# The compression operand laid out position by position and written by engines, and attention's order drawn from new seeds

## The chip, the cores and the metric

One core of a Trainium2 chip runs the whole program: two layers of a decoder trunk on 256 tokens of width 1024. The metric is the device time of one execution in microseconds (us), as the median of several runs. The engines are TensorE (PE in the profile, PEld for its weight loads), VectorE (DVE), ScalarE (ACT), GpSimd (POOL) and SyncE (SP), which in this kernel only issues DMAs. Each engine works through its own queue of instructions in the order in which the program emitted them, and waits by semaphores for the others.

## The reference, cut to what matters

Layer 0 is a recurrent mixer and an MLP, layer 1 is sparse attention and an MLP, and a norm follows. The change lies in layer 1's attention, in the compression of keys and values:

```python
def _compress(z, pe, w1, w2):                 # z: 256 tokens, 4 groups, 64 wide
    chunks = z.reshape(B, n_chunk, CMP_STRIDE, G, DH)                  # 16 chunks of 16 tokens
    blocks = jnp.concatenate([chunks[:, r:r + nc] for r in range(CMP_RATIO)], axis=2)   # 15 blocks of 32
    blocks = blocks + pe[None, None, :, None, :]
    flat = jnp.transpose(blocks, (0, 1, 3, 2, 4)).reshape(B, nc, G, CMP_LEN * DH)
    return jax.nn.gelu(flat @ w1, approximate=True) @ w2
...
    k_c = _compress(kv[:, :, 0], pe_k, w1_k, w2_k)
    v_c = _compress(kv[:, :, 1], pe_v, w1_v, w2_v)
...
        s_c = jnp.einsum('qghd,ngd->ghqn', qf, kc) - slopes * d_c.astype(jnp.float32)
        p_c = _masked_softmax(s_c, d_c >= 0)
        o_c = jnp.einsum('ghqn,ngd->qghd', p_c, vc)
...
        o = g[..., 0:1] * o_c + g[..., 1:2] * o_s + g[..., 2:3] * o_w
```

## The kernel before

The activations stay on chip, transposed: `xt` holds 8 chunks of 128 features by 256 tokens. Almost every product is taken as three passes over operands split into a high and a low part (`mm3`, L328 to L330), with a weight of 128 rows and 256 moving columns. Weights stream from memory in pieces of 128x1024 fp32: SP loads a piece into one of 5 raw buffers (L274), ACT or DVE casts the high part (L288, L336), DVE subtracts to get the low part (L297, L333). Seven split pieces are held in `whl`. Eight pieces of attention go another way, through POOL's queue: a DMA into the high part (L388), a negation (L390) and an accumulating DMA (L392).

The attention stage is a section of its own. `Section.add` records each operation with its engine (or a choice of two), an assumed duration, the keys that it reads and writes and a due time `t`. `Plan.emit` then sets the order: `priorities` adds random amounts to the due times, drawn from a list of seeds, a list schedule and six rounds of pushing work backwards and forwards follow, and the operations are emitted by the start times that come out. `HI` is such a choice: a copy or cast that ACT (0.31) or DVE (0.21) may do. So the seeds decide the order on all five queues, and which of ACT and DVE does a copy. The recurrent layer has seeds of its own; the MLPs are written in a fixed order.

The attention section projects, in this order, `ks0 kw0 q0 q1 ck0 ck1 cv0 cv1` (the early ones), then `q2`, the values `v` in 5 pieces (L1019 to L1021, which also give the branch gates `gts`), `q3 ks1 kw1 q4 q5 q6 q7`, and the output projection `o0`, `o1`. Between these stand the scores of 16 heads (L1149 and L1150 on PE, L1156 on DVE, the exponentials L1159 on ACT), the rescaling by the gates (L1178), transposes of the probabilities (L1189, with L1192 on ACT and L1193 on DVE), and their products with the values (L1214 to L1228). The chunks `q3` to `q7`, `ks1` and `kw1` are cast into one of two buffers `th`, and SP moves the halves to their partitions by DMA (L364); `tl` is the same for the low parts.

Compression: `cproj` projects `ck` and `cv` (two chunks of two groups each), multiplies by the norm's factor into `tt` (L943 on DVE), and lays the result out in `zf`, the moving operand of the first layer. `zf` has 122 columns, namely 2 (keys, values) times 60 blocks and one column with the position embedding, for each of 16 positions `l`; its upper 64 partitions hold the positions 16 to 31 of the block. In memory it is `(z l)`: a column's 16 positions lie side by side. One block of 64x240 is contiguous, and one DMA moves it: 16 in all, issued by SP (`sec.move`, L364, `zwoh<-tt` in the trace, since `zf` lies in the buffer `zwoh`). Two small DMAs bring the embeddings (L931). `hidden` then runs 16 fp32 products of 128x122, one per position, added up in one bank (L957), each reading `zf[:, :, l]`; ACT and DVE finish the gelu into `hid` (L963 to L971). `kc_out` (L978) and `vc_out` (L997) are the second layer, `compressed` the branch's scores, softmax and transposes (L1086 to L1130).

Of the kernel before, what the change touches and what calls it, by code (L numbers as in the profile page):

```python
# [28 lines left out]
NB = 15  # L29
# [4 lines left out]
LATE = "q2 v q3 ks1 kw1 q4 q5 q6 q7".split()  # L34
TE = 2.73
W1T, T1, TH, TC, T2, T3, THS, THD, THT, NEARLY = -3.89, 3.12, 0.0, 4.6, 4.94, 3.03, 13.46, 6.73, 5.46, 8
SEEDS, ROUNDS, SHIFT, MOVES, SPREAD = ((3,), (144, 22097, 77409, 21939, 78114, 80006, 60630, 7069, 62773, 82469, 25830, 79801, 92020, 84794, 19920, 86923, 46302, 34626)), 6, 1.5, 12, 3.0
HPEN, LPEN, APEN, LEAD = 0.56, 1.0, 0.0, 9.0
RPEN = 0.51
WARM = 16  # L40
# [47 lines left out]
class Plan:  # L88
# [8 lines left out]
    def add(self, eng, dur, fn=None, r=(), w=(), t=0.0, lag=None):  # L97

        if fn is None:
            eng, fn = eng, dur  # L100
        if isinstance(eng, str):
            eng = [(eng, dur, 0.0)]
        i, deps = len(self.tasks), set()
        for k in r:
            if k in self.writer:
                deps.add(self.writer[k])
            self.readers.setdefault(k, []).append(i)
        for k in w:
            deps.update(self.readers.pop(k, ()))
            if k in self.writer:  # L110
                deps.add(self.writer[k])
            self.writer[k] = i
        deps.discard(i)
        self.tasks.append((eng, fn, sorted(deps), t, lag))
# [124 lines left out]
def trunk_kernel(ctx: ExitStack, tc: tile.TileContext, x_in, vec_in, const_in, w2_in, wts, out):  # L239
    nc = tc.nc  # L240
    ctx.enter_context(tc.manual_schedule())
    pe, dve, act, pool = nc.tensor, nc.vector, nc.scalar, nc.gpsimd
# [92 lines left out]
    def copy(o, a):  # L335
        return lambda e: (e.copy if e is act else e.tensor_copy)(o, a)  # L336

    zcols = lambda x: x[:, :S]
    HI = [("act", 0.31, 0.0), ("dve", 0.21, APEN)]
# [139 lines left out]
    vec = consts.tile([P, V_N], F32, name="vec")  # L479
# [55 lines left out]
    with ExitStack() as ph:  # L535
        rg = ph.enter_context(tc.tile_pool(name="rg", bufs=1))
        sec = Section()
        add, table = sec.add, sec.table
# [18 lines left out]
        for x in FIRST.split():  # L557
            n = 1 + x.endswith("+")
# [18 lines left out]
        for k in range(KC):  # L577
            g = vec[:, V_GM + k:V_GM + k + 1]
            t = 0.6 * k - 3
            add("act", 0.4, lambda e, k=k, g=g: e.activation(hh[:, k], xt[:, k], AF.Identity, scale=g),  # L580
                r=[("xt", k), "vec0"], w=[("hh", k)], t=t)
            add("dve", 0.4, lambda e, k=k, g=g: e.scalar_tensor_tensor(
                hl[:, k], xt[:, k], g, hh[:, k].bitcast(F32), op0=OP.mult, op1=OP.subtract), r=[("xt", k), "vec0"],
                w=[("hh", k)], t=t)
# [3 lines left out]
        for q in range(4):  # L588
            for i in range(NFINE):
                w = slice(256 * q, 256 * q + 256)  # L590
                hi, lo, rw = hi_t[i][:, w], lo_t[i][:, w], raw_t[i][:, w]
                rk = [("raw0", i, q), ("raw", i)]
                t = 1.2 * q + 0.3 * i - 2.9
                add([("dve", 0.2, 0.0), ("act", 0.31, 0.5)], copy(hi, rw), r=rk, w=[("hi0", i, q)], t=t)
                add("dve", 0.34, diff(lo, rw, hi), r=rk + [("hi0", i, q)], w=[("lo0", i, q)],
                    t=t + 0.1)
        for a, b, n in ((0, 2, 2), (0, 1, 1), (4, 6, 2), (4, 5, 1), (0, 4, 1)):
            add("dve", 0.07 + 0.267 * n, lambda e, a=a, b=b, n=n: e.tensor_tensor(
                x2[:, a:a + n], x2[:, a:a + n], x2[:, b:b + n], op=OP.add), r=[("x2", b + i) for i in range(n)],
                w=[("x2", a + i) for i in range(n)], t=4 + a / 4)  # L600
# [6 lines left out]
        sp, nsp, e8, s8, s2, ac = many([P, 8], F32, "sp", 6)  # L607
# [146 lines left out]
        for m in range(8):  # L754
            wh, wl, wk = sec.weight("out", m, to + 2.65 * m)
            b = nextbank()
            z = sec.bank(("out", m), b, zcols)
# [6 lines left out]
            t = to + 2.65 * (m + 1)  # L764
# [55 lines left out]
    with ExitStack() as ph:  # L820
        at = ph.enter_context(tc.tile_pool(name="at", bufs=1))
        sec = Section()
        add, weight, proj_t, zview, table = sec.add, sec.weight, sec.proj, sec.bank, sec.table
        own_ = lambda hf: slice(hf * 64, hf * 64 + 64)
# [20 lines left out]
        zw = [at.tile([P, 8 * S], F32, name="zw" + n, tag=n) for n in ("oh", "ol")]  # L845
# [71 lines left out]

        pre = ph.enter_context(tc.tile_pool(name="ct", bufs=1))
        ZW = 61
        zf = zw[0][:, :2 * ZW * 16].rearrange("p (z l) -> p z l", l=16)  # L920
        w1 = zw[1].rearrange("p (l c) -> p l c", l=16)
        zok, wok = [("oh", j) for j in range(8)], [("ol", j) for j in range(8)]
        cb = pre.tile([P, 1], F32, name="cb")
# [4 lines left out]
        bd = osumt.rearrange("p a (j e) -> p a j e", j=4)  # L928
        for i in range(2):
            pecol = (V_PEK, V_PEV)[i]  # L930
            add("sp", 0.5, lambda e, i=i, c=pecol: e.dma_start(zf[:, ZW * i + 60], vec_in[:, c:c + 16]), r=zok,  # L931
                w=[("z", i, "p")], t=W1T, lag=2.0)
            o, ws = offs[-1] + 4 * P * 1024, slice(8 * i, 8 * i + 8)
            add("sp", 1.5, lambda e, o=o, ws=ws: e.dma_start(w1[:, ws], wts[o:o + P * 2048].rearrange(
                "(p l c) -> p l c", p=P, l=16)[:, ws]), w=wok[4 * i:4 * i + 4] + ["loads"], t=W1T, lag=2.0)
        add("pool", 0.15, lambda e: e.memset(hid, 0.0), w=["hid"], t=-5)

        def cproj(i, gp, b, t, step):
            z, zk = proj_t(("ck", "cv")[i], gp, b, t, step)
            t += 4 * step  # L940
            n = ti["n"] = ti["n"] + 1
            x, xk = tt[n % 3], ("tt", n % 3)
            add("dve", 0.34, lambda e: e.tensor_tensor(x, z(), rs, op=OP.mult), r=[zk, "rs"], w=[xk], t=t)  # L943
            for hf in range(2):
                g = gp * 2 + hf
                for j in range(2):
                    dst = zf[own_(j), ZW * i + g * NB:ZW * i + (g + 1) * NB].rearrange("p n l -> p (n l)")
                    sec.move(dst, x[own_(hf), j * 16:j * 16 + 240], [xk] + zok, [("z", i, g, j)], t + 0.5, "sp")

        def hidden(b, t):  # L950
            hp = zview("hp", b, lambda x: x[:, :2 * ZW])
# [282 lines left out]
        def out_t(half, m, b, t, step):  # L1234
            wh, wl, wk = weight("o%d" % half, m // 2, t)
            z = zview(("out", half, m), b, zcols)
            for ks in ((0, 1), (2, 3)) if half == 0 else ((0, 1), (2,), (3,)):
                def run(e, ks=ks):
                    for kk in ks:
                        o = (m % 2) * 512 + kk * P  # L1240
                        k = half * 4 + kk
                        mm3(z(), wh[:, o:o + P], wl[:, o:o + P], oh(k), ol(k), kk == 0, kk == 3)
                add("pe", 0.33 * len(ks), run, r=wk + [(n, half * 4 + kk) for n in ("oh", "ol") for kk in ks],
                    w=[("ps", b)], t=t)
                t += step * len(ks) / 2
            add("dve", 0.34, lambda e: residual(z(), m), r=[("ps", b)], w=[("xt", m)], t=t)
            return t
# [10 lines left out]
        for i, x in enumerate(EARLY):  # L1258
            te[x] = TE * i
            if x[0] == "c":  # L1260
                cproj("kv".index(x[1]), int(x[2]), i % 2, te[x], TE / 4)
            elif x[0] == "k":
                kchunk(int(x[2]), "sw".index(x[1]), i % 2, te[x], TE / 4)
            else:
                qchunk(int(x[1]), i % 2, te[x], TE / 4)
# [40 lines left out]
        for m in range(8):  # L1306
            t = out_t(1, m, (2, 3, 4, 0, 1)[m % 5], te - 2 + 1.4 * m, PJ)
# [133 lines left out]
```

## Time and profile before

| what | us |
|---|---|
| median of 3 runs | 585.29 (584.83 to 585.83) |
| the profiled execution | 585.05 |
| span of its trace | 583.3 |
| attention stage in it, from the norm's factor to the last product with the values | 269.9 to 390.3 |

The span is the stretch of the trace with work; 1.75 us of the profiled execution lie around it. Busy time of PE counts overlapping matmuls once, so a busy PE can still be slower than it could be; the distance between starts shows the pace. In the profile an fp32 product counts as two records, so the 16 products of `hidden` are 32 records on L957.

### The profile page before, as it was taken

The page shows a single profiled execution, that of the slowest core. Times are in us where ns is not written, and L with a number is a line of the kernel's source. Part 1 is how long each engine was busy: PE and PEld are TensorE (multiplying, and loading weights), DVE is VectorE, ACT ScalarE, POOL GpSimd, SP SyncE. Part 2 cuts the span into 40 slices and gives each one's busy share as a digit, 9 for nine tenths or more (in the row PEclk, how much of TensorE's full clock was granted, in tenths as well). Part 3 has the DMA queues.
Part 4 walks back from the last instruction along what each step waited for, and adds up shares of the span by engine and source line. Part 5 has one row for each costly group of instructions (what it writes and reads, how often), then busy time and mean ns, then how long its engine had stood idle before and what let it go on. Part 6 is the DMA issues. An engine that isn't in the chain of part 4 may idle for free.

```text
span 583.3 us, 12179 instructions
## 1 busy us (share of the span) xinstructions
PE 569.1 (98%) x4756; PEld 558.6 (96%) x4756; DVE 418.3 (72%) x862; ACT 354.6 (61%) x712; POOL 56.3 (10%) x69
## 2 busy tenths in 40 slices
PE   8999999999999999999999989999999999999994
PEld 7999999999999999999999988989999999999994
DVE  6999998767665645647749989999866766464432
ACT  7699674856654433437628999986865664343410
POOL 1200000000000112211011100000000000132320
PEclk8999999999999999999999999999999999999998
DMA  8943575656556565566496776433666767467402
GB/s 286 389 127 136 182 229 197 222 188 199 195 186 213 184 217 177 189 222 217 107 332 173 157 185 172 140 70 109 227 212 183 199 198 241 156 185 219 139 2 72
DMA packets 34617, 108.39 MB, mean 186 GB/s; under 512 B 4576, under 2 KB 8304, under 8 KB 34560
## 3 DMA queue, kind: packets, MB, share of 16 engines
q1 hardware_dynamic: 31632, 98.61, 51.6%
q0 software_dynamic: 2352, 8.49, 6.5%
q8 instruction: 37, 0.61, 0.4%
q10 hardware_dynamic: 576, 0.53, 0.3%
q14 instruction: 20, 0.16, 0.1%
HBM read 103.48 MB, written 1.05 MB: 179 GB/s over the span
## 4 chain that ended last, share of the span: by engine, by line
PE 88%; ACT 5%; DVE 4%; DMA 1%; issue 0%; SPq 0%; DVEq 0%; ACTq 0%
PE bank L328 27%; PE bank L329 26%; PE bank L330 26%; PE bank L690 2%; ACT pt L1159 2%; PE bank L957 1%; ACT pt L1178 1%; DMA raw<-in_dram 1%; PE bank L1189 1%; DVE ptl L1193 1%; PE bank L1019 1%; ACT pth L1192 1%; PE bank L1021 1%; PE bank L1020 1%; DVE pt L1156 1%
## 5 line engine op out<-in xcount | busy, mean ns | idle before, releaser
L328 PE MATMUL bank<-hhl,whl 128*128 128x256 f32 x768 | 215.2, 280 | 1.5 <-DVE whl L336 1.2
L330 PE MATMUL bank<-hhl,whl 128*128 128x256 f32 x768 | 213.3, 278 | 0.2 <-DVE whl L333 0.2
L329 PE MATMUL bank<-hhl,whl 128*128 128x256 f32 x768 | 212.9, 277 | 0.0
L297 DVE TENSOR_TENSOR whl<-raw,whl 128x1024 fp32r<-128x1024 f32 x118 | 147.5, 1272 | 2.7 <-ACT whl L288 2.7
L328 PEld LDWEIGHTS bank<-hhl,whl 128*128 128x128 f32 x768 | 144.8, 189 | 2.4 <-ACT whl L336 1.4
L330 PEld LDWEIGHTS bank<-hhl,whl 128*128 128x128 f32 x768 | 144.7, 188 | 0.7 <-DVE whl L333 0.6
L329 PEld LDWEIGHTS bank<-hhl,whl 128*128 128x128 f32 x768 | 144.9, 189 | 0.2
L328 PE MATMUL bank<-uhl,whl 128*128 128x256 f32 x512 | 141.4, 276 | 0.0
L330 PE MATMUL bank<-uhl,whl 128*128 128x256 f32 x512 | 141.3, 276 | 0.0
L329 PE MATMUL bank<-uhl,whl 128*128 128x256 f32 x512 | 141.3, 276 | 0.0
L288 ACT CAST whl<-raw 128x1024 fp32r<-128x1024 f32 x119 | 121.3, 1043 | 23.0 <-issue 18.8
L328 PEld LDWEIGHTS bank<-uhl,whl 128*128 128x128 f32 x512 | 96.1, 188 | 0.0
L329 PEld LDWEIGHTS bank<-uhl,whl 128*128 128x128 f32 x512 | 96.1, 188 | 0.0
L330 PEld LDWEIGHTS bank<-uhl,whl 128*128 128x128 f32 x512 | 96.1, 188 | 0.0
L532 DVE TENSOR_TENSOR xt<-xt,bank 128x256 f32<-128x256 f32 x40 | 16.1, 418 | 84.4 <-PE bank L330 84.4
L333 DVE TENSOR_TENSOR whl<-raw,whl 128x1024 fp32r<-128x1024 f32 (+3 forms) x64 | 66.5, 1060 | 5.3 <-ACT whl L336 5.2
L785 ACT ACTIVATE u<-t 128x256 f32<-128x256 f32 x64 | 26.7, 417 | 56.1 <-DVE t L780 55.5
L336 ACT CAST whl<-raw 128x1024 fp32r<-128x1024 f32 (+3 forms) x54 | 50.4, 952 | 14.1 <-DMA raw<-in_dram 9.4
L780 DVE SCALAR_TENSOR_TENSOR t<-bank,rstd 128x256 f32<-128x256 f32 x64 | 26.9, 423 | 42.9 <-PE bank L330 42.4
L1317 ACT ACTIVATE xg<-xt,vec 128x256 f32<-128x256 f32 x8 | 4.1, 510 | 47.9 <-DVE xt L532 47.9
L1159 ACT ACTIVATE pt<-pt,mx 128x256 f32<-128x256 f32 (+1 forms) x64 | 28.6, 448 | 3.4 <-DVE mx L1156 3.3
L502 POOL TENSOR_TENSOR acc<-xt 128x256 f32<-128x256 f32 x2 | 3.0, 1521 | 266.0 <-DVE xt L532 266.0
(207 smaller groups left out, 822.8 us busy)
## 6 DMA issues: line engine op xcount, KB each, us to landing
raw<-in_dram SPq DMA_DIRECT2D x167, 512.0 KB, 4.0
whl<-in_dram POOLq DMA_DIRECT2D x16, 512.0 KB, 5.8
gw<-in_dram SPq DMA_DIRECT2D x4, 512.0 KB, 8.4
raw<-in_dram SPq DMA_DIRECT2D x6, 256.0 KB, 5.6
xt<-in_dram SPq DMA_DIRECT2D x4, 256.0 KB, 5.5
zwol<-in_dram SPq DMA_DIRECT2D x2, 512.0 KB, 5.5
zwoh<-tt SPq DMA_DIRECT2D x16, 60.0 KB, 2.7
raw<-in_dram SPq DMA_DIRECT2D x2, 456.0 KB, 5.3
```

The lines of the kernel that those rows point to most:

```text
L288: (act.copy if eng is None else eng.tensor_copy)(hi_t[i % NSPL][:, :n], raw_t[i % NRAW][:, :n])
L297: (eng or dve).tensor_tensor(lo[:, :n], raw_t[i % NRAW][:, :n], hi[:, :n].bitcast(F32), op=OP.subtract)
L328: pe.matmul(ps, wh, xh, start=start, stop=False)
L329: pe.matmul(ps, wh, xl, start=False, stop=False)
L330: pe.matmul(ps, wl, xh, start=False, stop=stop)
L333: return lambda e: e.tensor_tensor(o, a, h.bitcast(F32), op=OP.subtract)
L336: return lambda e: (e.copy if e is act else e.tensor_copy)(o, a)
L532: dve.tensor_tensor(xt[:, m], xt[:, m], z, op=OP.add)
L690: e.matmul(z(), gw[b][:, o:o + P], xb[2 * b + k], start=k == 0, stop=k == 1)
L780: dve.scalar_tensor_tensor(t, z, 0.0, rs, op0=OP.max, op1=OP.mult)
L785: act.activation(u, t, AF.Square)
L1159: add("act", (0.39, 0.49)[qc], lambda e, row=row, j=j: e.activation(row, row, AF.Exp, bias=mx[:, j:j + 1], scale=-1.0, accum_out=sm[:, j:j ...
```

## The change

`zf` becomes `(l z)` in memory: the 122 columns of one position lie side by side, and a column's positions are 122 elements apart. A product then reads 122 adjacent elements of each partition; before, it read one element in 16. What was a contiguous 64x240 block to write is now 240 elements with the inner step over `l` of 122 elements, and the 16 DMAs become 16 copies on ACT or DVE, as `HI` chooses. The two embedding DMAs become two copies on POOL from `vec`, which is on chip already. The seeds of the attention section are another list of the same length.

```diff
-SEEDS, ROUNDS, SHIFT, MOVES, SPREAD = ((3,), (144, 22097, 77409, 21939, 78114, 80006, 60630, 7069, 62773, 82469, 25830, 79801, 92020, 84794, 19920, 86923, 46302, 34626)), 6, 1.5, 12, 3.0
+SEEDS, ROUNDS, SHIFT, MOVES, SPREAD = ((3,), (220, 33432, 96759, 54319, 81652, 71160, 78891, 31244, 32846, 69253, 85598, 41052, 13522, 40016, 76129, 88216, 44072, 68996)), 6, 1.5, 12, 3.0
...
-        zf = zw[0][:, :2 * ZW * 16].rearrange("p (z l) -> p z l", l=16)
+        zf = zw[0][:, :2 * ZW * 16].rearrange("p (l z) -> p z l", l=16)
...
-            add("sp", 0.5, lambda e, i=i, c=pecol: e.dma_start(zf[:, ZW * i + 60], vec_in[:, c:c + 16]), r=zok,
-                w=[("z", i, "p")], t=W1T, lag=2.0)
+            add("pool", 0.15, lambda e, i=i, c=pecol: e.tensor_copy(zf[:, ZW * i + 60], vec[:, c:c + 16]), r=zok + ["vec"],
+                w=[("z", i, "p")], t=-5)
...
-                    dst = zf[own_(j), ZW * i + g * NB:ZW * i + (g + 1) * NB].rearrange("p n l -> p (n l)")
-                    sec.move(dst, x[own_(hf), j * 16:j * 16 + 240], [xk] + zok, [("z", i, g, j)], t + 0.5, "sp")
+                    dst = zf[own_(j), ZW * i + g * NB:ZW * i + (g + 1) * NB]
+                    y = x[own_(hf), j * 16:j * 16 + 240].rearrange("p (n l) -> p n l", l=16)
+                    add(HI, copy(dst, y), r=[xk] + zok, w=[("z", i, g, j)], t=t + 0.5)
```

From L944 on the numbers of the lines shift by one, so the products of `hidden` are L957 before and L958 after.

Three places of the order follow; each row is one instruction (`x16`: 16 alike in a row). The first is PE's queue around `hidden`. Before, with the values' products (L1019 to L1021) around it:

```order
L1019 MATMUL bank_3597<-whl,hhl 128x304
L1020 MATMUL bank_3597<-whl,hhl 128x304
L1021 MATMUL bank_3597<-whl,hhl 128x304
L957 MATMUL bank_3641<-zwoh,zwol 128x122 x16
L1019 MATMUL bank_3612<-whl,hhl 128x304
```

Now, with the projection `q2` (into bank_3559) around it:

```order
L328 MATMUL bank_3559<-hhl,whl 128x256
L329 MATMUL bank_3559<-hhl,whl 128x256
L330 MATMUL bank_3559<-hhl,whl 128x256
L958 MATMUL bank_3591<-zwoh,zwol 128x122 x16
L328 MATMUL bank_3559<-hhl,whl 128x256
```

`hidden` moved from behind 10 groups of three value products to before the last quarter of `q2`; no value product stands ahead of it any more. PE has the same 4541 instructions in both kernels.

The second place is DVE's queue at the end of the early projections (tt_3214, tt_3215, tt_3216 are `ck1`, `cv0`, `cv1` there; L1156 and L1157 are the score rows). Before:

```order
L333 TENSOR_TENSOR whl<-raw_78,whl 128x1024
L333 TENSOR_TENSOR whl<-raw_79,whl 128x1024
L1156 ISA pt,mx_3238<-bank_3541,cst 128x256
L1156 ISA mx_3238 128x1
L1156 ISA pt,mx_3238<-bank_3541,cst 128x256
L1156 ISA mx_3238 128x1
L943 TENSOR_TENSOR tt_3216<-bank_3512,rstd 128x256
```

Now:

```order
L336 COPY zwoh<-tt_3215 64x15x16 x3
L1157 ISA pt,mx_3238<-bank_3530,cst 128x128
L1157 ISA mx_3238 128x1
L1157 ISA pt,mx_3238<-bank_3535,cst 128x256
L1157 ISA mx_3238 128x1
L1157 ISA pt,mx_3238<-bank_3535,cst 128x256
L1157 ISA mx_3238 128x1
L1157 ISA pt,mx_3238<-bank_3530,cst 128x128
L1157 ISA mx_3238 128x1
L943 TENSOR_TENSOR tt_3216<-bank_3505,rstd 128x256
L336 COPY zwoh<-tt_3216 64x15x16 x3
L333 TENSOR_TENSOR whl<-raw_79,whl 128x1024
```

Nine of the 16 copies are on DVE, three behind each of the last three chunks, and seven on ACT. Elsewhere in the section nine rescales (L1178) that ACT had are DVE's now, and seven casts that DVE had are ACT's. The four score rows of one head all stand ahead of `cv1`'s product now, and the second weight split stands behind the copies.

The third place is the cast into `th` for `q5`, on DVE before (th_3217):

```order
L1169 SCALAR_TENSOR_TENSOR sm_3244<-sm_3244,gri 128x4
L1228 TENSOR_TENSOR osum<-osum,bank_4118 64x256
L336 CAST th_3217<-tt_3216 128x256
L1171 RECIPROCAL sm_3244<-sm_3244 128x4
L1193 TENSOR_TENSOR ptl<-bank_4170,pth 128x384
```

Now on ACT, as is the cast for `q6` (th_3218):

```order
L1193 CAST pth<-bank_4201 128x384
L336 CAST th_3217<-tt_3216 128x256
L1193 CAST pth<-bank_4231 128x384
L390 ACTIVATE whl<-whl 128x1024
L336 CAST whl<-raw_81 128x1024
L1179 ACTIVATE pt<-pt,sm_3244 128x128
L1193 CAST pth<-bank_4258 128x384
L1179 ACTIVATE pt<-pt,sm_3244 128x256
L336 CAST th_3218<-tt_3214 128x256
```

What stands behind a cast that waits for a buffer is now ACT's work (here the high parts of transposed probabilities, L1193 after the shift) where it was DVE's.

## The prediction

> **What bounds the kernel now.** First the busy shares on the page, to see which engine fills the span.
>
> ```profile
> span 583.3 us, 12179 instructions
> ...
> PE 569.1 (98%) x4756; PEld 558.6 (96%) x4756; DVE 418.3 (72%) x862; ACT 354.6 (61%) x712; POOL 56.3 (10%) x69
> ```
>
> PE is busy 98% of the span, so a microsecond taken out of PE's queue shortens the kernel, unless something else is late there. The shares mix stages; the table of windows over the attention stage shows who is full when (columns: window, its length, then busy us of PE, PEld, DVE, ACT, POOL with instruction counts, granted clock, DMA share, GB/s).
>
> ```profile
> 100.00:150.00 50.00, 50.00 (x444) 50.00 (x443) 36.01 (x60) 32.77 (x62) 0.00 (x0) 1.00 0.63 208
> ...
> 280.00:290.00 10.00, 10.00 (x88) 9.91 (x87) 8.50 (x24) 5.37 (x17) 0.62 (x1) 1.00 0.44 120
> 290.00:300.00 10.00, 10.00 (x65) 9.96 (x65) 3.54 (x6) 2.80 (x9) 1.48 (x2) 1.00 1.01 335
> 300.00:310.00 10.00, 9.89 (x72) 9.69 (x71) 6.96 (x25) 3.88 (x12) 2.03 (x6) 1.00 1.04 281
> 310.00:320.00 10.00, 10.00 (x82) 9.62 (x82) 9.43 (x40) 9.53 (x27) 1.43 (x2) 1.00 0.59 145
> 320.00:340.00 20.00, 19.94 (x157) 18.91 (x156) 19.37 (x82) 19.60 (x67) 2.86 (x4) 1.00 0.76 182
> 340.00:350.00 10.00, 8.50 (x66) 7.96 (x65) 8.02 (x27) 8.78 (x25) 1.43 (x2) 1.00 0.60 134
> 350.00:370.00 20.00, 19.31 (x138) 16.86 (x137) 19.52 (x83) 19.93 (x61) 1.43 (x2) 1.00 0.70 197
> 370.00:388.00 18.00, 16.98 (x128) 15.15 (x127) 17.01 (x65) 17.82 (x59) 0.87 (x1) 1.00 0.18 41
> ```
>
> The first row lies in the MLP and gives the pace of a pass, 50 / 444 = 0.113 us. Attention has two stretches. Until 310 only PE is full: from 280 to 310 DVE is idle for 30 - 19.0 = 11.0 us and ACT for 30 - 12.05 = 17.95 us. From 310 to 388 all three are: ACT is busy 75.7 of 78 us, DVE 73.4, and PE loses 48 - 44.79 = 3.2 us from 340 on. The clock is at 1.00 throughout, so it plays no part.
>
> Next, the timeline of PE around `hidden`, and two other groups of fp32 products for its pace (start, busy, engine, line, tiles, shape, count).
>
> ```profile
> 28.32 1.89 PE L690 MATMUL bank<-xb,gw 128*128 128x256 f32 x8
> 29.86 0.47 PE L328 MATMUL bank<-hhl,whl 128*128 128x256 f32 x1
> ...
> 295.59 6.82 PE L957 MATMUL bank<-zwoh,zwol 128*128 128x122 f32 x32
> ...
> 302.06 0.49 PE L1019 MATMUL bank<-whl,hhl 128*128 128x304 f32 x1
> ...
> 307.92 1.00 PE L997 MATMUL bank<-w2raw,pt 128*128 128x64 f32 x8
> 308.73 0.37 PE L1086 MATMUL bank<-kc,sa 128*128 128x32 f32 x2
> ```
>
> From start to the start of what follows, a record of L957 takes (302.06 - 295.59) / 32 = 0.202 us. A record of L690 with 256 adjacent columns takes 1.54 / 8 = 0.193, one of L997 with 64 columns 0.81 / 8 = 0.101. So 122 columns at a step of 16 elements go as slowly as 256 adjacent ones. No row of this trace has another long strided operand, so that the step is the cause is an inference from these three groups.
>
> **The products, the one large term.** The change makes the 122 columns adjacent. Between L997 (0.101 at 64) and L690 (0.193 at 256) the price is either a floor with a slope (256 columns give 0.00075 each, 122 of them 0.092, below the floor of 0.101) or a straight line (0.129). I take the floor, since 64 columns at 0.00075 would be 0.048 and L997 does not go so low. 32 x 0.101 = 3.2 us in place of 6.5: **-3.2 us of PE**. The straight line gives 4.1 and -2.3; were the step not the cause, 0.
>
> [...]
>
> **The 16 copies.** No row writes single elements at a large step on ACT or DVE. The nearest are copies and subtractions of the same 64 partitions and size.
>
> ```profile
> L336 DVE CAST kh<-tt 64x256 fp32r<-64x256 f32 x1 | 0.3, 292 | 0.0
> L333 DVE TENSOR_TENSOR kl<-tt,kh 64x256 fp32r<-64x256 f32 x4 | 1.6, 417 | 0.0
> L336 ACT CAST kh<-tt 64x256 fp32r<-64x256 f32 x7 | 2.7, 405 | 0.6 <-DVE tt L893 0.5
> ```
>
> A DVE copy lies between 0.29 and 0.42; I take 0.35, the middle. ACT takes 0.41. Nine on DVE are 3.2 us, seven on ACT 2.9. Both fit the idle time from 280 to 310, but `hidden` now comes early and waits for the last of them, so DVE's chain has to be followed.
>
> ```profile
> 282.37 0.42 DVE L943 TENSOR_TENSOR tt<-bank,rstd 128x256 f32<-128x256 f32 x1 [0.77 <-PE bank L330]
> 282.71 1.80 DVE L333 TENSOR_TENSOR whl<-raw,whl 128x912 fp32r<-128x912 f32 x2
> 285.09 0.42 DVE L943 TENSOR_TENSOR tt<-bank,rstd 128x256 f32<-128x256 f32 x1 [0.58 <-PE bank L330]
> 285.43 2.35 DVE L333 TENSOR_TENSOR whl<-raw,whl 128x1024 fp32r<-128x1024 f32 x2
> ...
> 288.54 0.42 DVE L943 TENSOR_TENSOR tt<-bank,rstd 128x256 f32<-128x256 f32 x1
> 288.88 0.28 DVE L1156 CUSTOM_DVE_ANT_0 pt<-bank,cst 128x128 f32<-128x128 f32 x1
> ...
> 289.30 0.08 DVE L1156 DVE_READ_ACCUMULATOR2_ANT mx<- 128x1 f32 x1
> ...
> 291.51 0.48 DVE L871 SCALAR_TENSOR_TENSOR tt<-bank,cst,rstd 128x256 f32<-128x256 f32 x1 [1.54 <-PE bank L330]
> ```
>
> `q2` ends at PE near 291.3 here; `hidden` now starts a quarter of it earlier (6 passes of 0.113, 0.7 us), at 290.6. `cv1`'s product on DVE started at 288.54. Six copies stand ahead of it now (2.1 us), two more score rows (0.4, from 288.88 to 289.30), less the second weight split (half of 2.35, so -1.2), and 1.35 us of waiting for PE are there to fill: 288.54 + 2.1 + 0.4 - 1.2 - 1.35 = 288.5. With its 0.4 and three copies the operand is whole at 290.0, ahead of 290.6. **0, with 0.6 us in hand.** Without that cover each further 0.1 us per DVE copy makes the nine 0.9 us later, of which all but the first 0.6 fall on PE.
>
> [...]
>
> **What leaves SP's queue, and the rest.** SP issued the 16 moves in one piece and the weight loads stood behind them (the first row is from the waits, the others from the timeline).
>
> ```profile
> POOL whl L388 <- DVE tt L943: 22.5, 1, 22.5
> ...
> 279.92 11.46 SPq L364 DMA_DIRECT2D zwoh<-tt  x16
> 291.48 14.54 SPq L274 DMA_DIRECT2D raw<-in_dram  x7
> ...
> 296.24 1.05 ACT L336 CAST whl<-raw 128x1024 fp32r<-128x1024 f32 x1 [3.81 <-DMA raw<-in_dram]
> ```
>
> With them gone the loads go out as soon as buffers are free, and ACT's wait of 3.81 us at 296.24 should mostly go. PE did not wait for that piece (10.00 of 10 us busy), so this is worth 0 by itself. The two embedding DMAs leave SP too, ahead of any waiter: 0. POOL's two copies stand before its wait of 22.5 us for a buffer (L388): 0. Both kernels have the same 4541 instructions on PE, so no other PE term exists.
>
> **What the freed time meets.** `hidden` starts 5.0 us earlier (290.6 for 295.59) and lasts 3.2 less, so the gelu and the second layer run in the idle stretch, where ACT (5.15) and DVE (3.76) waited.
>
> ```profile
> 302.31 0.70 DVE L390 TENSOR_SCALAR whl<-whl 128x1024 fp32r<-128x1024 f32 x1 [3.76 <-DMA whl<-in_dram]
> 302.44 0.32 ACT L963 COPY cb<-bank 64x1 f32<-64x1 f32 x2 [5.15 <-PE bank L957]
> ```
>
> Work that now starts the full stretch is therefore ahead by at least what PE gains. Whether the new order loses more or less than the 3.2 us that PE waits from 340 to 388 can't be read from a list of seeds: bounded by all of it gone (-3.2) and doubled (+3.2). I take 0, since the counts on ACT and DVE behind `hidden` hardly change: nine rescales (L1178) pass from ACT to DVE, and some seven casts the other way.
>
> **The sum** against the profiled execution: 585.05 - 3.2 + 0 + 0 = 581.85. The median of the runs, 585.29, is 0.24 above that execution: **582.1 us**, 0.55% less.
>
> **The rivals.** *More:* the early compression takes load out of the full stretch, and PE's 3.2 us of waiting go with it: 585.3 - 6.4 = 578.9. For it speak the 11.0 and 17.95 idle us before 310; against it, that many of PE's waits have causes of their own, as the next one.
>
> *Slower, a cast that waits for a move.* These rows are DVE's and PE's timeline in the full stretch.
>
> ```profile
> 342.44 0.29 DVE L336 CAST th<-tt 128x256 fp32r<-128x256 f32 x1 [1.74 <-DMA sb<-th]
> ...
> 343.41 0.52 PE L1189 MATMUL bank<-cst,pt 128*128 128x128 f32 x3 [1.50 <-DVE ptl L1193]
> ```
>
> A cast into `th` waited 1.74 us until the move out of that buffer had landed; the subtraction behind it on DVE was late, and PE stood for 1.50 us. The new order puts the casts of `q5` and `q6` on ACT, busy 19.93 of 20 us there, with two casts of transposed probabilities (L1192) between them, for which PE waits. Each such wait costs 1.5. It is slower from the third new one on: 585.3 - 3.2 + 4.5 = 586.6. Two leave no change (585.1). For it: the same two buffers serve seven chunks in turn. Against it: it showed once, and SP's queue carries the same moves.
>
> *No change: copies at double price.* At 0.68 us, nine copies end 3.0 us later, the 0.6 in hand go, and PE waits 2.4: 585.3 - 3.2 + 2.4 = 584.5. [...] Slower than before only from 0.77 us per copy on (9 x 0.42 = 3.8 = 0.6 + 3.2). Against it: DVE's rows show at most 0.42 for this size. *Or the pace does not come from the step:* 585.3. Against that stand L690 and L997.
>
> **How the numbers follow.** Forecast -3.2, give or take 1: 0.50. More: 0.21. No measurable change, by either way: 0.16. Slower: 0.13. A measurement of this kernel tells about 0.2% (1.2 us) from no change. So faster 0.71, same 0.16, slower 0.13. The range reaches from the full rival (578.9, rounded down to 578.6) to no gain with the spread of the runs (585.5); outside lie most of the slower cases and a little below, near 0.15.
>
> **What would show it.** Right: L958's 32 records in 3.2 to 4.1 us, no wait ahead of them; copies of 0.29 to 0.42 us; SP without `zwoh<-tt`; `gts` ready 2 to 3 us earlier; PE's busy share from 340 on about as before. Wrong: records still 0.2 us apart; PE waiting for a copy before L958; copies of 0.6 us or more; more waits of L1189 or L1216 for casts and subtractions, above all behind a cast into `th`.

## The result, and the profile after

| | before | after |
|---|---|---|
| median of 20 runs each | 585.82 us | 597.63 us |
| all runs | 584.71 to 588.51 | 587.60 to 590.74 (7 runs), 595.50 to 600.58 (13 runs) |
| the profiled execution, its span | 585.05, 583.3 | 598.05, 596.2 |

The change made the kernel slower. The times of the changed kernel fall into two groups with nothing between 590.74 and 595.50; a run more than 1.5% above its kernel's fastest counts as slow, and the ratios in this document leave slow runs out, here 12 of the 13 in the upper group: 1.0072, 95% interval 1.0049 to 1.0095. Why there are two groups is the main finding below. The profiled execution is of the upper one. Its busy shares (engine, busy us, share of the span, instructions):

```profile
span 596.2 us, 12149 instructions
...
PE 578.4 (97%) x4756; PEld 568.0 (95%) x4756; DVE 424.9 (71%) x874; ACT 360.0 (60%) x716; POOL 57.5 (10%) x71
```

PE has as many instructions as before, and is busy 9.3 us longer. The table of windows of the changed kernel, for the attention stage and a piece of the second MLP (columns as in the prediction), and then the same last row of the kernel before:

```profile
280.00:290.00 10.00, 9.52 (x77) 9.20 (x75) 9.42 (x25) 8.89 (x20) 0.63 (x1) 1.00 0.46 148
290.00:300.00 10.00, 9.12 (x73) 8.99 (x74) 7.50 (x26) 4.92 (x17) 0.91 (x1) 1.00 0.84 249
300.00:310.00 10.00, 10.00 (x75) 9.67 (x75) 9.37 (x34) 5.96 (x17) 1.71 (x6) 1.00 0.47 126
310.00:320.00 10.00, 10.00 (x86) 9.91 (x85) 9.92 (x36) 9.88 (x26) 2.33 (x4) 1.00 0.88 216
320.00:340.00 20.00, 17.75 (x115) 16.81 (x115) 14.69 (x61) 13.66 (x43) 2.84 (x4) 0.83 0.82 174
340.00:350.00 10.00, 10.00 (x78) 9.45 (x78) 9.63 (x37) 9.85 (x30) 1.43 (x2) 1.00 0.60 138
350.00:370.00 20.00, 18.58 (x140) 16.92 (x139) 19.34 (x83) 19.68 (x64) 1.38 (x2) 1.00 0.70 199
370.00:388.00 18.00, 17.91 (x139) 16.61 (x136) 17.00 (x68) 17.29 (x60) 0.94 (x2) 1.00 0.19 30
...
450.00:500.00 50.00, 50.00 (x419) 50.00 (x418) 34.24 (x53) 28.51 (x50) 0.00 (x0) 1.00 0.62 188
```

```profile
450.00:500.00 50.00, 50.00 (x444) 50.00 (x443) 32.81 (x50) 28.29 (x48) 1.52 (x1) 1.00 0.62 197
```

The reader is to see three things. From 280 to 300 PE, which was full there before, loses 0.48 and 0.88 us. From 320 to 340 it makes 115 instructions where it made 157, at a mean clock of 0.83. And in the second MLP, where nothing was changed, PE counts as fully busy at a clock of 1.00, but makes 419 passes in 50 us where it made 444. The timeline of PE shows this as a pace: the starts of a line that comes every third pass lie 0.36 us apart, so a pass takes 0.1200; before it took 0.1133, as in the first MLP of both kernels.

```profile
430.06 0.28 PE L328 MATMUL bank<-hhl,whl 128*128 128x256 f32 x1
...
430.42 0.28 PE L328 MATMUL bank<-hhl,whl 128*128 128x256 f32 x1
```

This slow pace begins where PE takes up the MLP's passes behind L529, at the end of attention, and holds to the end. In PE's order 1488 passes stand behind that point: 1488 x 0.0067 = **10.0 of the 12.9 us** by which the span is longer. The other 2.9 arise before it.

The same pace stands in short stretches elsewhere, and not only behind a wait. The changed kernel has 72 passes at 0.1200 from 280 to 290, where the kernel before needs 0.114 a pass, which costs 0.4 us; the timelines of six other profiles of the new order, from 285 on, have 0.1194 to 0.1200 there. The passes follow score products of 512 columns with no idle time between:

```profile
286.97 0.39 PE L1151 MATMUL bank<-kl,sa 128*128 128x512 f32 x1
287.20 0.28 PE L328 MATMUL bank<-hhl,whl 128*128 128x256 f32 x1
...
287.56 0.28 PE L328 MATMUL bank<-hhl,whl 128*128 128x256 f32 x1
```

### The profile page after: what moved, and what is told of

Same layout as the page of the kernel before. It is cut to its first block, busy times and chain, and to the rows that moved or that the text cites. A ratio compares the mean times of both kernels' runs of the same rounds, so it can differ in the third digit from the quotient of the medians.

```text
span 596.2 us, 12149 instructions
## 1 busy us (share of the span) xinstructions
PE 578.4 (97%) x4756; PEld 568.0 (95%) x4756; DVE 424.9 (71%) x874; ACT 360.0 (60%) x716; POOL 57.5 (10%) x71
## 4 chain that ended last, share of the span: by engine, by line
PE 70%; DVE 17%; ACT 5%; DMA 4%; issue 2%; SPq 0%; POOL 0%; DVEq 0%; ACTq 0%; POOLq 0%
PE bank L329 22%; PE bank L328 21%; PE bank L330 21%; DVE whl L333 4%; DMA raw<-in_dram 2%; DVE xb L670 1%; ACT pt L1160 1%; DMA sa<-tl 1%; DVE ptl L1194 1%; ACT whl L336 1%; DMA xt<-in_dram 1%; DVE pt L1157 1%; ACT pt L1179 1%; DVE t L722 1%; PE bank L958 1%
## 5 line engine op out<-in xcount | busy, mean ns | idle before, releaser
L328 PE MATMUL bank<-uhl,whl 128*128 128x256 f32 x512 | 143.4, 280 | 0.0
L330 PE MATMUL bank<-uhl,whl 128*128 128x256 f32 x512 | 143.1, 279 | 0.0
L329 PE MATMUL bank<-uhl,whl 128*128 128x256 f32 x512 | 143.0, 279 | 0.0
L336 ACT CAST whl<-raw 128x1024 fp32r<-128x1024 f32 (+3 forms) x55 | 51.8, 956 | 10.7 <-DMA raw<-in_dram 6.9
```

The costliest lines, as they stand in the source:

```text
L328: pe.matmul(ps, wh, xh, start=start, stop=False)
L329: pe.matmul(ps, wh, xl, start=False, stop=False)
L330: pe.matmul(ps, wl, xh, start=False, stop=stop)
```

## Experiments: which half of the change loses

The theories at first: ORDER, that the new list of seeds loses the time, and COPIES, that the engines' copies do. The change has one line of seeds and some ten of layout, so each half runs alone.

**The new layout with the seeds of before.**

```diff
-SEEDS, ... = ((3,), (220, 33432, 96759, ...)), ...
+SEEDS, ... = ((3,), (144, 22097, 77409, ...)), ...
```

> The changed kernel with the seeds of before: same layout, same 16 copies, another order. Theory ORDER (the new seeds' order is what costs, by putting the moves of q3 behind weight loads, so that PE stands near 326 and its clock is halved): the products take 3.4 us, the copies 0.6 us each as in the changed kernel, no halved clock, 582 to 585 us, and no runs near 598. Rival COPIES (0.6 us copies on two full engines cost more than the products give): 587 to 590 us whatever the seeds.

Measured 585.0 (583.54 to 588.15) beside 586.23 for the kernel before in the same set: ratio 0.9977, interval 0.9960 to 0.9993. One group of times, and the old pace in the second MLP.

**The old layout with the new seeds** (the same line in the kernel before).

> The kernel before with the new seeds alone: old layout, moves by DMA, another order. ORDER: slower than before, 588 to 592 us or more, with PE idle around the first moves into sa and sb. COPIES: within 1.5 us of before (584.5 to 587).

Measured 597.45, ratio 1.0094 (1.0069 to 1.0120), in two groups: 590.68 to 592.68 and 602.22 to 603.63. The layout alone gains 1.2 us; the order alone loses.

**The exact order of the changed kernel with the old storage**, so that the copies write adjacent elements and the products read at a step of 16 again; and **the copies walked the other way** in the changed kernel.

```diff
-        zf = zw[0][:, :2 * ZW * 16].rearrange("p (l z) -> p z l", l=16)
+        zf = zw[0][:, :2 * ZW * 16].rearrange("p (z l) -> p z l", l=16)
```

```diff
-  dst = zf[own_(j), ZW * i + g * NB:ZW * i + (g + 1) * NB]
-  y = x[own_(hf), j * 16:j * 16 + 240].rearrange("p (n l) -> p n l", l=16)
+  dst = zf[own_(j), ZW * i + g * NB:ZW * i + (g + 1) * NB].rearrange("p n l -> p l n")
+  y = x[own_(hf), j * 16:j * 16 + 240].rearrange("p (n l) -> p l n", l=16)
```

> The changed kernel with the operand stored as before (one block of a copy contiguous, the products reading at a step of 16 elements); the order on every queue is that of the changed kernel, instruction by instruction. If the step of the read sets the pace of the products, its 32 records are again 0.20 us apart (6.5 us in all) instead of 0.107; if the step of the write sets the price of a copy, copies fall from 0.60 and 0.64 us to 0.29 to 0.42. ORDER: the stop near 326 stays, 588 to 592 us in runs without the slow pace, about 1 to 3 us above the changed kernel's fast runs. COPIES: faster than the changed kernel by 1 us or more.

> The changed kernel with the same layout and order, but each copy walks position by position: it writes runs of 15 adjacent elements and reads at a step of 16. If only writing at a step is dear, a copy takes 0.3 to 0.42 us and the products start 1 to 2 us earlier (290.6 to 291.5); if reading at a step is as dear, 0.6 us again. ORDER: 587 to 590 us, as the changed kernel's fast runs, and the halved clock stays. COPIES: 584 to 586 us.

Measured 592.91 (ratio 1.0070, 1.0044 to 1.0097) and 588.29 (1.0030, 1.0012 to 1.0049), each with both groups of times again (six of 12 runs from 594.56 to 601.40; four of 13 from 597.57 to 599.57). So either storage has them, and COPIES falls as the cause of the large loss. What the two do show is the price of a step. The groups of instructions of the changed kernel, of the old storage and of the other walk (busy us, mean ns of one):

```profile
L336 DVE COPY zwoh<-tt 64x240 f32<-64x240 f32 x9 | 5.3, 594 | 0.2
...
L336 ACT COPY zwoh<-tt 64x240 f32<-64x240 f32 x7 | 4.5, 638 | 1.2 <-DVE tt L943 1.1
L958 PE MATMUL bank<-zwoh,zwol 128*128 128x122 f32 x32 | 3.8, 277 | 0.6 <-DVE zwoh L336 0.6
```

```profile
L958 PE MATMUL bank<-zwoh,zwol 128*128 128x122 f32 x32 | 6.8, 384 | 0.0
...
L336 ACT COPY zwoh<-tt 64x240 f32<-64x240 f32 x7 | 2.7, 391 | 1.2 <-DVE tt L943 1.1
L336 DVE COPY zwoh<-tt 64x240 f32<-64x240 f32 x9 | 2.6, 288 | 0.2
```

```profile
L336 ACT COPY zwoh<-tt 64x240 f32<-64x240 f32 x7 | 4.4, 622 | 0.8 <-DVE tt L943 0.7
...
L336 DVE COPY zwoh<-tt 64x240 f32<-64x240 f32 x9 | 3.3, 368 | 0.2
```

The products take 3.8 us or 6.8 with the storage alone, all else equal. A copy on DVE takes 0.29 us into adjacent elements, 0.59 when each element written lies 488 bytes from the last, 0.37 when only the read has the step (64 bytes). On ACT a step on either side costs about the same: 0.39 without, 0.64 and 0.62 with. The two steps differ in size as well as in side, and no run here separates these.

## Experiments: what the slow pace is

Every kernel with the new order showed two more things that the old order's profiles did not: PE stops for 2.3 to 2.7 us for a move, somewhere between 327 and 352, and waits 0.17 us ahead of L529 for the norm's reciprocal, since DVE has it behind two weight splits. Behind the stop the granted clock is at 0.50 (from 329.25 in the changed kernel; in the windows from 352 to 358 in the old layout with the new seeds, where the stop was 2.48 us). The two splits and the wait:

```profile
405.35 2.35 DVE L333 TENSOR_TENSOR whl<-raw,whl 128x1024 fp32r<-128x1024 f32 x2
407.62 0.16 DVE L443 RECIPROCAL rcol<-rcol 128x2 f32<-128x2 f32 x1
```

```profile
407.84 0.43 PE L529 MATMUL bank<-cst,rcol 128*128 128x128 f32 x2 [0.17 <-DVE rcol L443]
```

The theories now: CLOCK, that the halved clock leaves the slow pace behind, and BREAK, that the pace is a state of PE's stream which its last interruption leaves, by chance the one or the other. Three kernels tell them apart.

**Small interruptions in the second MLP.**

```diff
                     wh, wl = get("up%d" % layer, m)
+                    if layer == 1 and m in (8, 16, 24):
+                        pe.matmul(bank(7)[:, :1], ident, ones, start=True, stop=True)
 ...
                 for j in range(4):
+                    if layer == 1 and j == 0 and m in (2, 5):
+                        pe.matmul(bank(7)[:, :1], ident, ones, start=True, stop=True)
```

> The changed kernel with one product of a single column put into PE's stream ahead of pieces 8, 16 and 24 of the second MLP's first layer and ahead of outputs 2 and 5 of its second, to break the stream there. Each costs about 0.2 us, 1 us in all. Theory BREAK (the slow pace of the second MLP, 0.1200 us a pass for 0.1133, is a state that the last interruption of PE's stream leaves behind, by chance the one or the other): the pace changes at these products and nowhere else, in the profile some of the six segments run at 0.113 and others at 0.120, and the times spread over 588 to 599 with values between the two groups. Theory CLOCK (the slow pace is left behind by the halved clock near 330 and stays to the end): one pace from 408 to the end, and two groups of times as before, near 590 and 599, with nothing between.

**The reciprocal moved ahead of the two splits**, in the changed kernel. DVE's order, the only one that differs:

```diff
 L467 TENSOR_TENSOR acc<-acc,sq_99 128x256
-L333 TENSOR_TENSOR whl<-raw_81,whl 128x1024
-L333 TENSOR_TENSOR whl<-raw_79,whl 128x1024
 L443 RECIPROCAL rcol<-rcol 128x2
+L333 TENSOR_TENSOR whl<-raw_81,whl 128x1024
+L333 TENSOR_TENSOR whl<-raw_79,whl 128x1024
```

> The changed kernel with one instruction moved: DVE's reciprocal of the norm (rcol, L443) stands ahead of the two weight splits that it stood behind, so PE no longer waits 0.17 us for it ahead of L529. All else stands as in the changed kernel, PE's stop of 2.3 us near 327 for the move of q3 and the halved clock behind it with it. Theory BREAK with this wait as the break: no slow pace in the second MLP, every run in the lower group, 587 to 591, median 588.5. Theory CLOCK: the wait is beside the point, half of the runs or more stay in the upper group, median 590 to 598.

**The mirror of it**: the new layout in the old order, with the reciprocal behind one split more.

```diff
 L333 TENSOR_TENSOR whl<-raw_79,whl 128x1024
+L333 TENSOR_TENSOR whl<-raw_80,whl 128x1024
 L443 RECIPROCAL rcol<-rcol 128x2
-L333 TENSOR_TENSOR whl<-raw_80,whl 128x1024
```

> The mirror of it: the new layout with the order of before (585.0, pace 0.1133, no wait ahead of L529), and one instruction moved, a DVE weight split of 1.2 us put ahead of the reciprocal, so that PE waits 0.2 to 0.4 us for it ahead of L529. Nothing stops PE near 327 and the clock stays at 1.00. Theory BREAK: about half of the runs go to the slow pace, 160 us by 5.8% or 9 to 10 us, so two groups near 585.3 and 595. Theory CLOCK: one group at 585.2 to 585.5.

The windows of the first of them, ahead of its first small product (at 425.84) and behind it:

```profile
410.00:420.00 10.00, 10.00 (x87) 10.00 (x87) 7.45 (x12) 8.37 (x16) 0.00 (x0) 1.00 0.85 302
430.00:440.00 10.00, 10.00 (x91) 10.00 (x90) 6.70 (x11) 6.23 (x11) 0.00 (x0) 1.00 0.58 194
```

Behind a product of one column the slow pace ended: 0.1178 us a pass up to it and for ten passes behind it, 0.1133 from 427.24 on, and 443 passes in the 50 us from 450 and from 500. All five runs lie at 590.04 to 591.02; the upper group is gone. BREAK had expected the later products to bring the slow pace back at times, which none did. In the second kernel the profile has no wait at L529, the pace is 0.1133 throughout the second MLP, and the runs lie at 587.08 to 589.07 (ratio 1.0038, 1.0023 to 1.0052; one further run took 2200 us, which nothing here explains). The stop and the halved clock are still in that profile, so CLOCK falls.

The third kernel gave two groups, 583.93 to 586.70 and 590.56 to 592.28, six runs each, as BREAK had it, though 5.5 us apart where 9 to 10 were expected. The wait came out shorter than meant: in its profiles L529 starts 0.28 to 0.32 us after the product before it, which is 0.12 without a wait and 0.45 in the changed kernel. Its profile was of the lower group, so it ran three times more.

> The kernel of the old order with the reciprocal behind a third split once more, for its profile alone: its runs fell into two groups, 583.9 to 586.7 and 590.6 to 592.3, and the profile taken was one of the lower group, at 0.1134 us a pass. By BREAK a run of the upper group shows a pace of 0.120 from the restart at L529 on, at a clock of 1.00, up to some later break (5.5 us more are 95 us of it, not the whole region); a run of the lower group shows nothing new.

> The old order with the reciprocal behind a third split, for its profile. By BREAK a run of the upper group (590.6 to 592.3) shows 0.120 us a pass from the restart at L529 at a clock of 1.00, for 95 us if it costs 5.5; a run of the lower group shows 0.1134 all along.

> The same once more, since half of the runs are of the lower group.

They took 585.15, 592.52 and 592.43. The granted clock in slices of the span of the second, from its page, and one of its windows:

```profile
PEclk9999999999999999999999999999999999999997
```

```profile
450.00:500.00 50.00, 50.00 (x427) 50.00 (x426) 32.47 (x50) 27.65 (x48) 0.00 (x0) 1.00 0.64 201
```

Its clock was full up to the last slice, which begins at 575.9, PE waited at most 1.03 us at a time from 285 to 580, and still the second MLP runs slow from L529 to the end: 427 passes in 50 us. The timeline gives 0.1178 a pass, so there is more than one slow pace (0.1178 here, 0.1200 in the changed kernel). From L529 to the end of the span this run takes 183.8 us, and the profile of the lower group 177.6. So the smaller step of 5.5 us is not a shorter slow stretch, as the expectation had it, but a milder pace. What decides between the two paces is not shown: the kernel with the small products has the changed one's order up to L529, and had 0.1178. Nor does the length of the wait alone decide whether the pace is slow: in the four profiles of this kernel L529 starts 0.30 and 0.32 us after the product before it and leaves 0.1133, or 0.31 and 0.28 and leaves 0.1178.

Over all runs, without the kernel with the small products and the run of 2200 us: kernels with this wait ahead of L529 were in an upper group in 34 of 66 runs; those without it in 4 of 72, and the kernel before in none of 113. These four (one of the kernel with three edits, three of the one with short accumulating loads, both below) suggest that the wait is not the only way in; none of them was profiled. The run of 592.52 shows the slow pace beginning elsewhere too: in the first layer, behind a product that started 0.51 us after the one before it, the passes run at 0.1200 from 72.25 (at 0.1133 again from 110.03). What in PE's stream holds the pace stays open.

## Experiments: what stops PE near 327

This loss shows in PE's timeline and in the windows behind it, in the changed kernel:

```profile
329.41 0.80 PE L1150 MATMUL bank<-kh,sa 128*128 128x512 f32 x1 [2.25 <-DMA sa<-tl]
```

```profile
328.00:330.00 2.00, 0.59 (x1) 0.50 (x2) 1.53 (x3) 0.00 (x0) 0.00 (x0) 0.81 1.28 283
330.00:332.00 2.00, 2.00 (x11) 1.90 (x9) 0.94 (x5) 1.57 (x4) 0.22 (x1) 0.50 0.53 107
332.00:334.00 2.00, 2.00 (x11) 2.00 (x12) 1.39 (x8) 1.32 (x7) 0.65 (x1) 0.50 0.59 95
334.00:336.00 2.00, 2.00 (x9) 1.81 (x9) 0.35 (x3) 0.41 (x2) 0.00 (x0) 0.50 1.09 190
```

PE stands 2.25 us for a move of `q3`, and the clock is at 0.50 for 6.8 us, from 329.25 to 336.08. (In the windows of four other profiles, behind stops of 1.89 to 2.48 us, it is halved for 3.4 us; in those of the kernel with the small products, behind a stop of 3.15, for 6.8.) The question is why the move lands late. Its four moves, from 316 to 331, in the changed kernel and in the kernel before (count, size, us from issue to landing):

```profile
sa<-th SPq DMA_DIRECT2D x1, 64.0 KB, 6.6
sb<-th SPq DMA_DIRECT2D x1, 64.0 KB, 6.9
sa<-tl SPq DMA_DIRECT2D x1, 64.0 KB, 6.6
sb<-tl SPq DMA_DIRECT2D x1, 64.0 KB, 7.2
```

```profile
sa<-th SPq DMA_DIRECT2D x1, 64.0 KB, 1.9
sb<-th SPq DMA_DIRECT2D x1, 64.0 KB, 2.0
sb<-tl SPq DMA_DIRECT2D x1, 64.0 KB, 4.9
sa<-tl SPq DMA_DIRECT2D x1, 64.0 KB, 4.6
```

**One move late by hand**, in the new layout with the old order: `sa<-tl` behind the moves of the next chunk in SP's queue.

```diff
-L364 DMA sa_3204<-tl_3219 64x256
 ...
 L364 DMA kh<-th_3218 64x256 x2
+L364 DMA sa_3204<-tl_3219 64x256
 L274 DMA raw_80<-in_dram 128x1024
```

> The new layout with the order of before, and one move issued later: the transfer of q3's low halves into sa, issued at 322.3 and needed by PE at 327.1, stands six moves further back in SP's queue and is issued near 326.7, to land near 330.5. PE should stop for about 3.4 us, with no wait ahead of L529. If a stop of more than 2 us halves the clock: 0.50 for some 6 us behind it, 3 us more, 585.0 + 3.4 + 3 = 591.4; if it does not, 588.4. Theory CLOCK: half of the runs go to the slow pace as well, near 600. Theory BREAK: one group, since the stream restarts at L529 without a wait.

Measured 584.88 (0.9991, 0.9978 to 1.0003). The move went out at 326.64 as meant, but landed in 2.0 us, with the DMA engines 0.48 busy from 326 to 328; PE stopped for 0.86 us, and the clock stayed at 1.00. This did not test what it was made for; it shows that place in the queue alone did not make this move slow.

**A weight load taken out of its way**: on the kernel with the reciprocal moved, the second of two loads of 512 KB goes behind the moves (`raw_80`, which the old order has there too).

```diff
-L274 DMA raw_80<-in_dram 128x1024
 L364 DMA sa_3204<-th_3217 64x256
 ...
 L364 DMA kh<-th_3218 64x256 x2
+L274 DMA raw_80<-in_dram 128x1024
```

> The kernel with the reciprocal moved (588.1 in its median without the one run of 2200), and one more instruction moved: the second of two weight loads of 512 KB that SP issues at 315 and 318, ahead of q3's four moves of 64 KB at 321 to 324, stands behind them, next to last of the moves of the key chunk, where the order of before has it. Theory QUEUE (the moves land late because they stand behind bytes already queued on the DMA engines; 512 KB less at 210 GB/s are 2.4 us): they land 4 to 5 us after issue in place of 6.7 to 7.3, PE's stop of 2.44 us at 330 shrinks below 0.6, the clock stays at 1.00 there, and with 3 us of halved clock gone too the time is 588.1 - 2.4 - 3 = 582.7. Theory SHARE (POOL's accumulating weight loads, 0.5 MB each at 318.3, 320.6 and 323.8, make them late by themselves): landing stays above 6 us, stop above 2 us, clock halved, 587 to 588.5. Third: the load itself comes late and PE waits for its weights, with no gain.

Measured 588.0 (1.0035, 1.0022 to 1.0048); without the edit the six runs have their middle at 587.8 (the expectation's 588.1 is 0.3 too high). The moves still took 5.6 to 7.0 us, the stop was 2.38, the clock fell. QUEUE falls for this load. (The expectation counts three accumulating loads; the third, at 323.8, is a plain one.)

**POOL's accumulating loads cut to an eighth**, on the same kernel without the last edit.

```diff
-  e.dma_start(lo, src, accum_op=OP.add)
+  e.dma_start(lo[:, :128], src[:, :128], accum_op=OP.add)
```

> The kernel with the reciprocal moved (588.1), and POOL's accumulating weight loads (the low halves of eight weight pieces) cut from 1024 columns to 128, 64 KB in place of 512 each; the other 896 columns of these eight low halves are left out, so the output is not the reference's. Theory SHARE: with 0.9 MB less beside them q3's moves land in under 4.5 us, PE's stop of 2.4 us near 329 shrinks below 0.6, the clock stays at 1.00, and the time falls by 2.4 and the 1.7 us of the halved clock to 584.0 or less. Rival: the moves land late for another reason (the order of SP's queue, the plain loads), the stop stays above 2 us and the time above 587.

Here the moves and PE's windows were:

```profile
sa<-th SPq DMA_DIRECT2D x1, 64.0 KB, 2.6
sb<-th SPq DMA_DIRECT2D x1, 64.0 KB, 2.4
sa<-tl SPq DMA_DIRECT2D x1, 64.0 KB, 2.0
sb<-tl SPq DMA_DIRECT2D x1, 64.0 KB, 4.3
```

```profile
326.00:328.00 2.00, 2.00 (x17) 1.91 (x17) 2.00 (x8) 1.75 (x3) 0.00 (x0) 1.00 0.96 277
328.00:330.00 2.00, 2.00 (x20) 2.00 (x19) 2.00 (x10) 1.86 (x4) 0.51 (x1) 1.00 0.51 105
```

The moves land in 2.0 to 4.3 us, the stop and the halved clock are gone, and nine of 12 runs lie at 582.0 to 584.8 (median of all 582.86; ratio 0.9971, 0.9947 to 0.9996). So the accumulating loads are what makes the moves late, as SHARE had it: in the changed kernel two of them go out at 317.75 and 319.99, just ahead of the moves (the kernel before has one there, at 313.60). The kernel before shows the same further on, where nothing was edited: behind its accumulating loads of 327.30 and 330.40, two moves issued at 333.06 and 333.57 take 7.4 and 8.2 us. Whether they hold a move up by their bytes alone or because they accumulate is not separated: this edit takes 0.9 MB out of the moves' way, the one before took 0.5.

This kernel leaves 3.7 MB of loads out and is no candidate. It gives the price of the stop with what it brings: 5.0 us by the runs (587.8 against 582.8, the middle of the nine). The two profiles, whose PE makes the same instructions in the same order, show where: the lead of the kernel with short loads is 0.3 us up to the stop, 2.9 after it, 4.5 after the 3.4 us of halved clock, and 4.6 at L529. Against the changed kernel, whose clock was halved for 6.8 us, the same count gives 2.4 for the stop and 3.0 for the clock, 5.4 in all.

## Experiments: two versions

**The old order with the other walk of the copies**, and **the new order with three edits** (reciprocal, weight load, walk).

> The new layout with the order of before (585.0), and the 16 copies walked the other way: runs of 15 adjacent elements written, read at a step of 16. DVE's nine copies should take 0.37 us in place of 0.60, 2.1 us less ahead of the product of hidden; ACT's seven stay near 0.62. In the kernel before this one PE waits 1.06 us for DVE ahead of a score at 289.8 and 0.37 for a copy ahead of hidden at 292.0. If the copies' price is what these waits come from, both shrink by 1.0 to 1.4 in sum: 583.6 to 584.0. If they come from the order of the work round them, 585.0.

> All three edits on the changed kernel: the reciprocal ahead of the weight splits, the second weight load behind q3's moves, and the copies walked in runs of 15. By QUEUE 582.7 less 1.0 to 1.4 for the cheaper copies, 581.3 to 581.7, faster than before by 0.7%; by SHARE 586 to 587.

Measured 584.40 (ratio 0.9981, 0.9967 to 0.9995) and 584.36 (0.9979, 0.9956 to 1.0001), beside 585.99. Neither is measurably better than the layout alone. In the first, DVE's copies took 0.37 us, both of PE's waits ahead of `hidden` went, and it began at 290.67. But the waits came back just behind it, in PE's timeline:

```profile
290.67 3.73 PE L958 MATMUL bank<-zwoh,zwol 128*128 128x122 f32 x32
...
298.08 0.41 PE L979 MATMUL bank<-hid,w2raw 128*128 128x64 f32 x2 [0.41 <-PE bank L1022]
...
300.43 1.08 PE L998 MATMUL bank<-w2raw,pt 128*128 128x64 f32 x8 [0.62 <-DVE kc L984]
```

PE now reaches the second layer before its operand is there, and in the profiled run (586.37) the clock was at a mean of 0.60 from 302 to 306 behind these two waits. In the second, the stop was still 1.89 us, with the clock halved behind it, so QUEUE's 581.3 to 581.7 was not reached; SHARE's 586 to 587 missed it on the other side.

## Why the prediction was wrong

Forecast 582.1, measured 597.63, above the range.

- **The products: right.** 3.2 to 4.1 us, by 0.101 a record; measured 3.6, from L958's start at 292.72 to the start of the next row at 296.29, 0.11 a record, for 6.5 before. The step of the operand was the cause: with the old storage alone the products took 6.8 again.
- **The 16 copies: the chain right in kind, the price too low, and one wait left out.** Taken at 0.35 and 0.41; measured 0.59 and 0.64. The operand was to be whole at 290.0, 0.6 us ahead of `hidden`; `hidden` began at 292.72 instead of 290.6. PE waited 0.72 us for DVE at 290.24 and 0.64 for the last copy, 1.36 us. That is the rival of copies at double price (which gave 2.4 at 0.68 each, a price that no row of the kernel before shows), and the same two waits, 1.43 us there, left 1.2 of the 3 us in the kernel with the old seeds (585.0). But the price is only part of it. With DVE's copies at 0.37 in the same order `hidden` began at 291.60, still 1.0 late, and at 290.67 only in the old order. The chain took DVE's 1.35 us of waiting as free for copies; in that kernel DVE stood 1.00 us at 285.88 for a weight cast by ACT, whose own copies took 0.62, and `cv1`'s product came at 289.75 where the chain had 288.5.
- **SP's queue and POOL's copies: 0, right as far as seen.** No PE wait in the profile names them.
- **What the freed time meets: the step that failed.** It said that work would be ahead by at least what PE gains, that the order's effect could not be read from a list of seeds, and took 0 between -3.2 and +3.2. The last gate values (`gts`) came 2.0 us later than before (308.91 for 306.90), not 2 to 3 earlier. The rival had the right transfers, the moves of `q3` and its followers out of the buffers `th` and `tl`; but what it charged was a cast waiting for a buffer, 1.5 us each, while PE itself waited for a move that landed late, and 2.25 us of waiting became 5.4 with the clock. What the rival *More* hoped for came in part: PE's waits from 340 to 388 fell from 3.2 us to 48 - 46.5 = 1.5. And it bounded the order by waits in attention alone: the far larger loss, 10.0 us, lies in a stretch whose instructions the change does not touch, at PE's full busy share, set off, in 13 of 20 runs, by a wait of 0.17 us at L529. Without that loss the time would still have been above the range: the lower group lies at 587.60 to 590.74.
- **The sum, put right.** Ahead of the restart, from the rows of the profile: -2.9 for the products, +1.4 for the waits ahead of `hidden`, +2.25 for the stop, about +3 for 6.8 us at half clock, -1.7 for the waits from 340 to 388, +0.2 at L529: 2.2 of the 2.9 us that are lost there. Of the other 0.7, 0.4 are the slow pace from 280 to 290, and the rest is in no single row. Behind it 10.0. The kernels give the same by other means: 582.8 with short accumulating loads, free of both losses, 5.0 for the stop and its clock, 10.0 for the pace are 597.8, beside 598.05 for the profiled execution. That 582.8 is 2.6 below the kernel before in its set, near the 3.2 that the forecast had, but in part by luck: the waits ahead of `hidden` cost 1.4 that it did not have, and the waits from 340 on fell by 1.7 that it did not count on.

## What to carry to other kernels

Where PE is the bound, its busy share does not show its pace (50.00 of 50 us busy at 419 passes as at 444 here): count passes in equal windows of an untouched stretch, and look at the last thing that interrupted the stream before it, since a wait of 0.17 us there cost 10 in more than half of the changed kernel's runs (13 of 20). An order found by search is to be judged by many runs, and by which transfers it puts just ahead of a small one that PE needs. When a layout moves a step from a reader to a writer, price the writer first (on DVE 0.59 us for 0.29 of the adjacent copy here, and 0.37 walked so that the writes run on).

## What the runs showed of the hardware that was not expected

- **A pace of TensorE that lasts.** In the second MLP passes of 256 columns ran at 0.1133, 0.1178 or 0.1200 us at a granted clock of 1.00, the last two unchanged for 170 us (0.1200 from 408.46 to 583.42 in the changed kernel, 0.1178 from 407.60 to 577.90 in the run of 592.52). A slow pace began behind a wait (0.17 us in the changed kernel), or behind products of 512 columns without one (0.1200 from 280.03, where the kernel before has 0.1133 from 280.13), and it ended ten passes behind a product of one column in the one profile that has it.
- **The clock falls behind a stop, and not by its length alone.** In attention it was halved (0.50 granted) for 3.4 us behind stops of 1.89 to 2.48 us, for 6.8 us behind stops of 2.25 and 3.15, and once for 3.4 us behind waits of 0.41 and 0.62 us within 3 us, but stayed at 1.00 behind one of 1.50 in the kernel before.
- **Moves of 64 KB beside accumulating loads.** 6.6 to 7.2 us from issue to landing behind two accumulating loads of 512 KB in the changed kernel, 2.0 to 4.3 with these cut to 64 KB in the kernel with short ones.
